# Seven FFN operand blocks at seven byte offsets: 128, 144, ... 224 behind a multiple of 256 in place of 192 for all

## The chip, the cores and the metric

The kernel runs on one core of a Trainium2 chip. The metric is the time of one execution on the device in microseconds (us). The operands lie in SBUF, the on-chip memory with 128 partitions; "an operand begins n bytes behind a multiple of 256" is said of its place within each partition. TensorE multiplies a stationary operand (128 x 128, the weights, loaded by an instruction of its own) by a moving one (128 partitions x 256 or 512 columns here) and adds the product up in PSUM. ScalarE (ACT in the profile) and VectorE (DVE) convert, add and multiply; GpSimd (POOL) and SyncE (SP) mostly issue DMAs.

## The reference, cut to what matters

One layer over 512 latent tokens of width 1024, behind a context of 256 tokens: a mixer (pooling and a two-way mLSTM), then a SwiGLU feed-forward network (FFN) of inner width 2816, then a last norm. The part in question is the FFN's first product:

```python
def _swiglu(h, w_in, w_out):
    g, u = jnp.split(h @ w_in, 2, axis=-1)
    return (jax.nn.silu(g) * u) @ w_out

x = x + g2 * _swiglu(_modulate(x, norm_ffn[l], sh2, sc2), w_ffn_in[l], w_ffn_out[l])
```

Here h is 512 x 1024 and w_in 1024 x 5632, all float32.

## The kernel before

Everything is kept transposed: features on the partitions (eight k tiles of 128), tokens in the columns, in two halves of 256. A float32 product is made of three matmuls of a faster type (float32r): each operand is split into a high part (a rounded copy) and a low one (the rest), and `mm3` (L180 to L186) issues, for each k tile, high weights by high tokens (L184), high weights by low tokens (L185) and low weights by high tokens (L186). The weights are the stationary operand, the tokens the moving one.

The FFN's inner width is cut into 22 blocks of 128 gate and 128 up columns. The first three blocks are computed directly (`Half`, L1126): for each half of the tokens, eight k tiles by three matmuls for the gate and as many for the up part. Blocks 3 to 21 go through a Strassen-Winograd scheme over 2 x 2 parts (gate and up by the two halves of the k tiles, and these by the two halves of the tokens): seven products in place of eight. `front` (L1046) and `back` (L1065) issue them, four k tiles by three matmuls each: twelve matmuls of 256 columns per product. `strassen` (L1080) interleaves the front of a block with the back of the block before; the weights of the next block are loaded, split and combined meanwhile by `prepare` (L997). In between, after blocks 7, 14 and 21, the second FFN product runs over the finished blocks (`ffn_out`, L1217), in matmuls of 512 columns, of 256 in the last round.

The moving operands of the Strassen products are the seven blocks that the change moves. B11, B21 and B22 are parts of the normed tokens (first half of the tokens with the upper and the lower four k tiles, second half with the lower four); N1, N2, T3 and T4 are sums and differences of such parts. Each is 128 x 1024, that is four k tiles of 256 columns, `kt(q, k)` (L944). All seven lie one behind the other in one tile, and there are two such tiles, `hp` (L940), one for the high parts and one for the low ones. `tl` aligns a tile to LINE = 256 bytes, and NEXT = 48 floats, 192 bytes, are left free at its beginning; a block is 4096 bytes long, so all seven, and each of their k tiles, begin 192 bytes behind a multiple of 256. The fourth part, B12, lies in tiles of its own (`act`, L1121) that begin on a multiple of 256. The direct blocks read the same operands: B11 and B21 for the first half of the tokens, B12 and B22 for the second (`hpart`, L947).

The blocks are written once, between the norm and the first Strassen product: B11, B21 and B22 by `norm_rest` (L957: ScalarE the high part at L960, VectorE the low one at L963), the others by `total` (L978) with casts and subtractions of 512 columns (`split`, L172). The order of TensorE's, ScalarE's and VectorE's work is written out by hand (`manual_schedule`), and nothing in it depends on where an operand begins. The filling matmuls before the last norm (`dense`, L1250) read B11 as both operands.

The stationary operands of the Strassen products are 128-column parts of the tiles wh, wl, gh, gl, oh and ol. All of these begin on multiples of 256 and a part is 512 bytes long, so the stationary operand always begins on a multiple of 256 there.

Of the kernel before, what the change touches and what calls it, by code (L numbers as in the profile page):

```python
# [11 lines left out]
F32R = mybir.dt.float32r  # L12
# [5 lines left out]
P = 128  # L18
D = 1024
# [13 lines left out]
LINE = 256  # L33
NEXT = 48
# [15 lines left out]
def layer_kernel(ctx: ExitStack, tc, xT, cT, w0, w1, wv0, wv, wada_a, wada_b, par, crow, bg, wpool,  # L50
# [17 lines left out]
    def tl(tag, shape, dtype=F32, bufs=1, align=None):  # L68
        cnt[0] += 1
        return homes[tag].tile(shape, dtype, name=f"{tag}_{cnt[0]}", tag=tag, bufs=bufs, align_bytes=align)  # L70
# [866 lines left out]

    hp = [tl("hp", [P, NEXT + 7 * D], F32R, 2, LINE) for _ in range(2)]  # L940
    B11, B21, B22, N1, N2, T3, T4 = ([t[:, NEXT + i * D:NEXT + (i + 1) * D] for t in hp] for i in range(7))
    B12 = None

    def kt(q, k):  # L944
# [429 lines left out]
```

## Time and profile before

| what | us |
|---|---|
| median of three timed runs | 891.28 |
| lowest and highest of them | 890.16, 891.31 |
| profiled execution, its own time | 892.56 |
| its span, first to last instruction | 890.8 |
| direct blocks 0 to 2 and writing of the hp tiles, about | 527 to 566 |
| Strassen products of blocks 3 to 7, with a change to the second FFN product after them | 566 to 618 |
| Strassen products of blocks 8 to 14 | 662.6 to 733 |
| Strassen products of blocks 15 to 21 | 770.5 to 839 |

The profile is of one execution. In its views, a group of instructions is given by line, engine, operation and tile (out<-in), with the number (x), the busy time, the mean duration of one in ns and the idle time before them. A timeline row has the start in us, the duration in us, engine, line, operation and tiles. The duration of a matmul reaches from its start to its modelled end; matmuls overlap, so the next one starts long before that, and what counts for the time is the distance from start to start, called the pace here. PEclk is the clock that TensorE was granted, in tenths of full speed on the page and as a share in the windows view.

### The profile page before, as it was taken

What the parts mean: (1) busy time and instruction counts of PE and PEld (TensorE: products, weight loads), DVE (VectorE), ACT (ScalarE), POOL (GpSimd) and SP (SyncE); (2) the same over time, 40 slices, a digit from 0 to 9 for tenths busy, and PEclk for the clock granted to TensorE, in tenths of its full rate; (3) what the DMA queues carried; (4) which work ended last, traced back from release to release, by engine and by line L of the source; (5) the groups of instructions that cost most, each with busy time, mean ns of one, the idle gap of its engine ahead of it and who ended that gap; (6) DMA issues with size and microseconds to landing.
All of it is one profiled execution on the core that took longest, in us unless ns stands there. A gap on an engine that the chain in (4) does not pass through costs nothing.

```text
span 890.8 us, 15038 instructions
## 1 busy us (share of the span) xinstructions
PE 879.4 (99%) x5920; PEld 801.3 (90%) x5920; DVE 613.4 (69%) x1187; ACT 434.7 (49%) x823; POOL 66.6 (7%) x93
## 2 busy tenths in 40 slices
PE   9999999999999999999999999999999999999996
PEld 7689798899888998889988899999889998899996
DVE  4678676868876787667886667884386743867644
ACT  4464363545345453354544456763156732666541
POOL 0000010010000100001000000110011100111000
PEclk9999999999999999999999999999999999999998
DMA  9853031435252632525343920574256643766402
GB/s 349 322 190 114 27 69 61 166 118 167 91 182 71 201 115 76 181 79 166 130 148 102 315 86 24 134 184 110 90 158 150 164 96 101 189 146 141 118 1 95
DMA packets 41445, 120.87 MB, mean 136 GB/s; under 512 B 4480, under 2 KB 8864, under 8 KB 40352
## 3 DMA queue, kind: packets, MB, share of 16 engines
q1 hardware_dynamic: 35904, 109.96, 38.2%
q0 software_dynamic: 5472, 9.96, 6.8%
q8 instruction: 46, 0.75, 0.3%
q14 instruction: 23, 0.19, 0.1%
HBM read 116.22 MB, written 3.69 MB: 135 GB/s over the span
## 4 chain that ended last, share of the span: by engine, by line
PE 89%; DVE 5%; ACT 3%; DMA 2%; issue 1%; DVEq 0%; SPq 0%; ACTq 0%
PE ps L184 20%; PE ps L186 20%; PE ps L185 20%; PE pat L334 3%; PE ps L566 3%; PE ps L565 3%; PE ps L567 3%; PE pat L781 2%; PE pat L780 2%; PE pat L779 2%; PE pat L184 2%; PE pat L185 2%; PE pat L186 2%; PE ps L334 1%; PE pat L740 1%; PE pat L739 1%
## 5 line engine op out<-in xcount | busy, mean ns | idle before, releaser
L184 PE MATMUL ps<-a,wh 128*128 128x512 f32 (+1 forms) x368 | 138.9, 377 | 0.0
L185 PE MATMUL ps<-a,wh 128*128 128x512 f32 (+1 forms) x368 | 138.5, 376 | 0.0
L186 PE MATMUL ps<-a,wl 128*128 128x512 f32 (+1 forms) x368 | 138.3, 376 | 0.0
L154 ACT CAST wh<-wr 128x1024 fp32r<-128x1024 f32 (+3 forms) x78 | 78.8, 1010 | 116.1 <-PE ps L185 88.2
L155 DVE TENSOR_TENSOR wl<-wr,wh 128x1024 fp32r<-128x1024 f32 (+3 forms) x78 | 91.8, 1177 | 44.4 <-ACT wh L154 43.3
L186 PEld LDWEIGHTS ps<-a,wl 128*128 128x128 f32 x368 | 69.3, 188 | 12.5
L184 PEld LDWEIGHTS ps<-a,wh 128*128 128x128 f32 x368 | 69.3, 188 | 12.2
L185 PEld LDWEIGHTS ps<-a,wh 128*128 128x128 f32 x368 | 69.3, 188 | 11.8
L186 PE MATMUL ps<-act,wl 128*128 128x512 f32 (+1 forms) x224 | 77.9, 348 | 0.6 <-DVE wl L155 0.6
L184 PE MATMUL ps<-act,wh 128*128 128x512 f32 (+1 forms) x224 | 77.9, 348 | 0.0
L185 PE MATMUL ps<-act,wh 128*128 128x512 f32 (+1 forms) x224 | 77.7, 347 | 0.0
L566 PE MATMUL ps<-wl,a 128*128 128x256 f32 (+1 forms) x192 | 54.5, 284 | 0.0
L567 PE MATMUL ps<-wh,a 128*128 128x256 f32 (+1 forms) x192 | 54.3, 283 | 0.0
L565 PE MATMUL ps<-wh,a 128*128 128x256 f32 (+1 forms) x192 | 54.3, 283 | 0.0
L1013 POOL DMA_DIRECT2D ol<-in_wffi x38 | 33.4, 888 | 258.0 <-ACT ol L1012 88.5
L184 PE MATMUL ps<-hp,gh 128*128 128x256 f32 x176 | 50.1, 285 | 1.2 <-ACT pat L1051 1.2
L1222 DVE SCALAR_TENSOR_TENSOR x<-ps,lb,x 128x512 f32<-128x512 f32 (+1 forms) x32 | 19.6, 616 | 45.6 <-PE ps L186 45.6
L184 PE MATMUL ps<-hp,oh 128*128 128x256 f32 x176 | 49.4, 280 | 0.1
L186 PE MATMUL ps<-hp,gl 128*128 128x256 f32 x176 | 49.2, 279 | 0.0
L185 PE MATMUL ps<-hp,gh 128*128 128x256 f32 x176 | 49.2, 279 | 0.0
L185 PE MATMUL ps<-hp,oh 128*128 128x256 f32 x176 | 49.1, 279 | 0.0
L186 PE MATMUL ps<-hp,ol 128*128 128x256 f32 x176 | 49.0, 279 | 0.0
(323 smaller groups left out, 2529.6 us busy)
## 6 DMA issues: line engine op xcount, KB each, us to landing
wr<-in_w SPq DMA_DIRECT2D x42, 512.0 KB, 3.5
pb<-in_wada_b SPq DMA_DIRECT2D x32, 512.0 KB, 4.2
wr<-in_wffi SPq DMA_DIRECT2D x25, 512.0 KB, 4.5
ur<-in_wffi SPq DMA_DIRECT2D x19, 512.0 KB, 3.9
ol<-in_wffi POOLq DMA_DIRECT2D x38, 256.0 KB, 4.9
ada<-in_wada_a SPq DMA_DIRECT2D x8, 1024.0 KB, 9.8
wr<-in_wffo SPq DMA_DIRECT2D x16, 448.0 KB, 3.5
wr<-in_wout SPq DMA_DIRECT2D x8, 512.0 KB, 3.5
```

What stands on the lines that cost most here:

```text
L154: nc.scalar.copy(wh, raw[:, :n])
L155: V.tensor_sub(wl, raw[:, :n], wh.bitcast(F32))
L184: nc.tensor.matmul(dst, wh, ah, start=first and i == 0, stop=False, skip_group_check=on)
L185: nc.tensor.matmul(dst, wh, al, start=False, stop=False, skip_group_check=on)
L186: nc.tensor.matmul(dst, wl, ah, start=False, stop=last and i == n - 1, skip_group_check=on)
L334: nc.tensor.matmul(acc0[i], w_first[k][i][w], aT[k][x], start=k + w + x == 0, stop=k == KT - 1 and w == 1)
L565: nc.tensor.matmul(acc[:, :n], ah, wh, start=kk == 0, stop=False)
L566: nc.tensor.matmul(acc[:, :n], ah, wl, start=False, stop=False)
L567: nc.tensor.matmul(acc[:, :n], al, wh, start=False, stop=kk == KT - 1)
L779: nc.tensor.matmul(o, sh_, vh[:, s, :], start=n == 0, stop=False)
L1013: nc.gpsimd.dma_start(l, dram, accum_op=ALU.add)
L1222: V.scalar_tensor_tensor(x1[j][:, c], acc[:, c], g2[:, j:j + 1], x1[j][:, c], ALU.mult, ALU.add)
```

## The change

The tile grows to 32 + 7 x 1028 floats, and block i begins at float 32 + 1028 i in place of 48 + 1024 i. In bytes that is 128 + 4112 i: with i from 0 to 6, B11 begins 128 bytes behind a multiple of 256, B21 144, B22 160, N1 176, N2 192, T3 208 and T4 224. The four k tiles of a block are 1024 bytes apart, so each has its block's offset. The high and the low tile change alike. Lengths, order, instructions and what is computed stay.

```diff
-    hp = [tl("hp", [P, NEXT + 7 * D], F32R, 2, LINE) for _ in range(2)]
-    B11, B21, B22, N1, N2, T3, T4 = ([t[:, NEXT + i * D:NEXT + (i + 1) * D] for t in hp] for i in range(7))
+
+    hp = [tl("hp", [P, 32 + 7 * (D + 4)], F32R, 2, LINE) for _ in range(2)]
+    B11, B21, B22, N1, N2, T3, T4 = ([t[:, o:o + D] for t in hp] for o in range(32, 7 * (D + 4), D + 4))
     B12 = None
```

## Prediction, on record before the result

> **What bounds the kernel now.** I read the page first: busy time, the clock in 40 slices, the chain that ended last.
>
> ```profile
> span 890.8 us, 15038 instructions
> PE 879.4 (99%) x5920; PEld 801.3 (90%) x5920; DVE 613.4 (69%) x1187; ACT 434.7 (49%) x823; POOL 66.6 (7%) x93
> PEclk9999999999999999999999999999999999999998
> PE 89%; DVE 5%; ACT 3%; DMA 2%; issue 1%; DVEq 0%; SPq 0%; ACTq 0%
> ```
>
> TensorE is busy 99% of the span, at the full granted clock, and 89% of the chain is its. A busy TensorE is not yet one at its best pace, though, so the second question is how far apart its matmuls start. The change touches only operands in the two hp tiles. The windows view, once for the matmuls that read hp and once for all matmuls in other stretches, gives length, busy time and (x) how many matmuls lie in each stretch:
>
> ```profile
> core 0: us, PE busy (x), PEclk, DMA share, GB/s
> 566.00:590.00 24.00, 22.80 (x192) 1.00 0.85 203
> 590.00:618.00 28.00, 28.00 (x240) 1.00 0.51 128
> 662.60:733.00 70.40, 69.92 (x588) 1.00 0.56 136
> 770.50:773.20 2.70, 2.67 (x23) 1.00 0.54 146
> 773.50:809.30 35.80, 35.80 (x312) 1.00 0.65 153
> 809.50:839.00 29.50, 29.50 (x252) 1.00 0.51 116
> ```
> ```profile
> 676.00:726.00 50.00, 50.00 (x427) 1.00 0.60 141
> 776.00:789.00 13.00, 13.00 (x117) 1.00 0.59 131
> 509.00:522.00 13.00, 13.00 (x111) 1.00 0.39 142
> 62.00:78.00 16.00, 16.00 (x129) 1.00 0.42 140
> ```
>
> And the groups of these stretches, by form, for the duration of one (in this order: 670 to 730, 776 to 789, 509 to 522, 62 to 78 us):
>
> ```profile
> L186 PE MATMUL ps<-hp,gl 128*128 128x256 f32 x48 | 13.5, 281 | 0.0
> L184 PE MATMUL ps<-hp,gh 128*128 128x256 f32 x12 | 3.3, 276 | 0.0
> L186 PE MATMUL ps<-act,ol 128*128 128x256 f32 x21 | 5.9, 283 | 0.0
> L566 PE MATMUL ps<-wl,a 128*128 128x272 f32 x43 | 12.5, 290 | 0.0
> ```
>
> A matmul is counted in a window when any part of it lies there, so with W the window and d one duration the pace is (W + d) / x. From 676 to 726 us: (50 + 0.281) / 427 = **117.8 ns**. From 776 to 789: (13 + 0.276) / 117 = **113.5 ns**. These are the same matmuls on the same operands (moving operand 192 bytes behind a multiple of 256, stationary one on the multiple); no wait lies in either. The duration tells the two apart: 281 ns against 276. From 509 to 522, where the moving operand is an act tile and begins on the multiple as the stationary one does: (13 + 0.283) / 111 = **119.7 ns**. So what bounds this stage is the pace, and the pace depends on where the operands begin, with two values for one and the same pair of places.
>
> When does it change? Around 809 us the pace turns from the fast to the slow one, at a matmul that started late:
>
> ```profile
> 809.19 0.28 PE L185 MATMUL ps<-hp,wh 128*128 128x256 f32 x1
> 809.31 0.28 PE L186 MATMUL ps<-hp,wl 128*128 128x256 f32 x1
> 809.43 0.38 PE L184 MATMUL ps<-hp,gh 128*128 128x256 f32 x1
> 809.65 0.28 PE L185 MATMUL ps<-hp,gh 128*128 128x256 f32 x1
> ```
>
> It starts 0.12 us after its forerunner, lasts 0.38, and the next comes 0.22 later. The stretch after it is slow, (29.5 + 0.281) / 252 = 118.2 ns with that stop. So the pace is held until something disturbs it, and the disturbance picks it anew.
>
> **The change part by part.** Nothing is added or taken away: the same instructions, semaphores and DMAs. In each hp tile block i of the seven moves from 192 bytes behind a multiple of 256 to 128 + 16 i. In a row's bytes the tile grows from 28,864 to 28,912; both round up to 113 x 256, so I take the tiles to begin where they did.
>
> First, the writes into hp (12 conversions of 256 columns and 8 casts of 512 on ScalarE, as many subtractions on VectorE). The same form into an act tile, on the multiple of 256, beside it:
>
> ```profile
> L960 ACT ACTIVATE hp<-tmp,lb 128x256 fp32r<-128x256 f32 x9 | 4.5, 495 | 0.0
> L960 ACT ACTIVATE act<-tmp,lb 128x256 fp32r<-128x256 f32 x4 | 2.0, 504 | 0.1
> L963 DVE SCALAR_TENSOR_TENSOR hp<-tmp,lb,hp 128x256 fp32r<-128x256 f32 x12 | 5.8, 483 | 0.4 <-ACT hp L960 0.3
> L963 DVE SCALAR_TENSOR_TENSOR act<-tmp,lb,act 128x256 fp32r<-128x256 f32 x4 | 1.9, 479 | 0.2 <-ACT act L960 0.2
> ```
>
> 495 against 504 and 483 against 479 ns: 9 ns either way over 20 writes is 0.2 us on an engine beside the path. Cost: nothing.
>
> Second, the matmuls. In the planned stage (blocks 3 to 21 of the first FFN product, 19 turns of seven products of twelve) 1596 matmuls read hp. Today one offset serves all seven products, so nothing but a stop disturbs a pace once taken. After the change the offset moves at every product: in the order of the trace B22 160, B21 144, T4 224, B11 128, N1 176, T3 208, N2 192, back to 160. The trace has one place where the offset moves every twelve matmuls at this width: the gate and up products of the second half, where the first four k tiles lie in act tiles (on the multiple) and the last four in hp (192 behind):
>
> ```profile
> 545.76 0.28 PE L186 MATMUL ps<-act,gl 128*128 128x256 f32 x1
> 545.88 0.29 PE L184 MATMUL ps<-hp,gh 128*128 128x256 f32 x1
> 546.00 0.28 PE L185 MATMUL ps<-hp,gh 128*128 128x256 f32 x1
> 546.12 0.28 PE L186 MATMUL ps<-hp,gl 128*128 128x256 f32 x1
> 546.24 0.28 PE L184 MATMUL ps<-hp,gh 128*128 128x256 f32 x1
> 546.35 0.28 PE L185 MATMUL ps<-hp,gh 128*128 128x256 f32 x1
> ...
> 547.26 0.28 PE L184 MATMUL ps<-act,gh 128*128 128x256 f32 x1
> ...
> 548.68 0.29 PE L184 MATMUL ps<-hp,gh 128*128 128x256 f32 x1
> ```
>
> The hp dozen takes 547.26 - 545.88 = 1.38 us, **115.0 ns** each: some starts 0.12 apart, then (546.35 to 547.26, eight starts) 0.91 / 8 = 113.8. The change of offset has brought it into the fast pace, at the cost of a few matmuls. The dozen on the multiple takes 548.68 - 547.26 = 1.42, 118.3 each, on its way to the 119.7 above.
>
> If every product after the change behaves as that hp dozen, the sum over the planned stage is: the slow matmuls, 240 + 588 + 23 + 252 = 1103, go from 117.8 to 115.0, 1103 x 2.8 = **3.1 us less**; the 312 of 773.5 to 809.3 go from 113.5 to 115.0, **0.5 us more**; the first 192, a mixture with stops, stay. Net **2.6 us less**. The bounds of the unknown: the six new offsets are in no row at this width. Below, every matmul at the fast pace with nothing lost at the changes: 1103 x 4.3 = 4.7 us less. Above, every matmul at the 119.7 of the operands that begin alike: 1103 x 1.9 + 312 x 6.2 + 192 x 3.4 (taking that mixture at 116.3) = 4.7 us more. I take the value between, from the hp dozen, since it is the nearest row: same width, same tile, same dozen.
>
> (The windows hold 1607 matmuls in all, since one that lies across an edge, or of the direct blocks before 566, is counted too.) The cover for a faster TensorE is there: in the stage that ran fast, the other engines had room.
>
> ```profile
> 770.00:809.00 39.00, 39.00 (x337) 38.44 (x336) 29.35 (x47) 26.46 (x47) 6.11 (x7) 1.00 0.65 155
> ```
>
> VectorE 29.35 and ScalarE 26.46 of 39 us; next to be late is ScalarE's copy at L1051, which TensorE waited for twice, 1.2 us in all, between 556 and 840 us:
>
> ```profile
> PE ps L184 <- ACT pat L1051: 1.2, 2, 0.9
> ```
>
> The 17 filling matmuls at L1253 use B11 for both operands and stay alike; 0.
>
> A rule that speaks against the whole change: the Trainium skill, page "TensorE: Matmul & The Clock Gate", section "Step-by-step: what each phase is for", has TensorE read SBUF through two independent ports, so that loading the next weights takes no read bandwidth from the running matmul. By that rule the place of the operands is of no account and the sum is 0. The trace speaks against it with its 119.7, 117.8 and 113.5 ns.
>
> **The time.** The profiled execution took 892.56 us for its span of 890.8; less 2.6 it is 889.96. It lies 1.28 above the median of the timed runs, 891.28, and I carry the difference over to that: 891.28 - 2.6 = **888.7 us**.
>
> **The rivals.**
>
> *Slower: the products never settle, or settle badly.* Each change of offset costs, and dozens are too short, or an offset such as 128 has only the pace of operands that begin alike. For it: where the offset moves every three matmuls (62 to 78 us, 272 columns) the pace is (16 + 0.290) / 129 = 126.3, against 113.5 x 272 / 256 = 120.6 for the fast pace at that width, 5.7 more and never settled; and the act dozens above went up from the fast pace. Against it: the hp dozens did settle. Price: 113.5 + 5.7 = 119.2 for all, 1103 x 1.4 + 312 x 5.7 + 192 x 2.9 = 3.9 us more, **895.2 us**; at 119.7 it is 4.7 more, 896.0. It decides when over half of the matmuls are slow: with the start of a dozen as above and the rest at 117.8, a product costs 115.0 + 8 x 4.3 / 12 = 117.9, no better than today's slow pace, and the 312 at 113.5 lose theirs: 312 x 4.4 = 1.4 us more, 892.7.
>
> *No change.* Half of the products settle fast and half slowly, or the offsets do not matter and only stops do. Pace (115.0 + 117.9) / 2 = 116.45: 1103 x 1.35 = 1.5 less, 312 x 2.95 = 0.9 more, **890.7 us**; if nothing depends on the offset, 891.3. For it: both paces occur on one offset. Against it: the three values above.
>
> *The change does not do what it says.* If the tile did not begin on a multiple of 256, the offsets would be others; the row grows within its rounding, so I give this no chance of its own.
>
> **How the numbers follow.** Settling fast, 888.7 us: 0.42, by itself 886.6 (891.28 - 4.7, nothing lost at the changes) to 889.5. No change: 0.26. Slower: 0.32. A measurement of this kernel can tell about 0.2%, 1.8 us, from no change, so faster means under 889.5, slower over 893.1: 0.42, 0.26, 0.32. Cases of both signs hold most of the chance, so the range reaches from 886.3 to 895.8 and leaves some 0.05 out below and 0.10 above.
>
> **What would show it.** In the groups by form, the durations of the hp matmuls in the planned stage: 276 after the first few of each dozen if I am right, 281 or 283 in whole products if the rival is. Product by product, the start of one dozen to the start of the next: 1.36 to 1.38 us if fast, 1.41 slow, 1.44 as with operands that begin alike. If long stretches of all seven products keep 117.8 as they do now, the change of offset does not pick the pace anew, and the mechanism is wrong. More waits for L1051 than 1.2 us would show that the gain is spent there.

## The result: 892.88 us, slower by 0.34%

| | median us | lowest, highest | runs |
|---|---|---|---|
| kernel before, beside the changed one | 890.09 | 888.98, 891.31 | 7 |
| changed kernel | 892.88 | 892.53, 894.13 | 7 |

The ratio is 1.0034, with a 95% interval from 1.0022 to 1.0046. The profiled execution of the changed kernel took 892.77 us, its span 891.0. That is only 0.21 us more than the profiled execution of the kernel before, 892.56: the 2.79 us stand between the medians, and why the two profiles lie so near to each other comes out further down.

The page of the changed kernel, the lines that answer to those shown of before:

```profile
span 891.0 us, 15038 instructions
PE 880.9 (99%) x5920; PEld 803.4 (90%) x5920; DVE 613.7 (69%) x1187; ACT 435.6 (49%) x823; POOL 66.8 (7%) x93
PEclk9999999999999999999999999999999999999999
PE 91%; DVE 4%; ACT 2%; issue 2%; DMA 0%; DVEq 0%; POOLq 0%; POOL 0%; ACTq 0%
```

Same number of instructions, same granted clock: the distances between the matmuls' starts are left to explain, that is the pace and the stops. The windows of the planned stage, for the matmuls that read hp (length, busy time, number), as in the prediction:

```profile
566.00:590.00 24.00, 23.41 (x198) 1.00 0.86 217
590.00:618.00 28.00, 27.34 (x232) 1.00 0.46 116
662.60:733.00 70.40, 68.78 (x580) 1.00 0.56 134
676.00:726.00 50.00, 50.00 (x427) 1.00 0.59 139
773.50:809.30 35.80, 35.80 (x305) 1.00 0.65 149
811.00:833.00 22.00, 22.00 (x189) 1.00 0.48 109
```

From 773.5 to 809.3 us the profile of before had 312 matmuls, this one has 305: that stretch went from 113.5 ns to about 118. From 676 to 726 nothing changed (427 and 427), because before had 117.8 there. From 566 to 590 the changed kernel even fits in six more, 198 for 192: TensorE was busy with them for 23.41 us there and for 22.80 before, so it lost less to stops. By the next stage it was 1.1 us ahead (first matmul at 661.45, before at 662.59), which is why 590 to 618 and 662.6 to 733 count fewer.

One turn of the changed kernel, the first matmul of each product from the timeline (B11, N1, T3, N2, then N2's seventh matmul, B22, B21, T4 and the next B11), each with its own offset:

```profile
677.49 0.28 PE L184 MATMUL ps<-hp,oh 128*128 128x256 f32 x1
...
678.93 0.28 PE L184 MATMUL ps<-hp,gh 128*128 128x256 f32 x1
...
680.35 0.28 PE L184 MATMUL ps<-hp,wh 128*128 128x256 f32 x1
...
681.78 0.28 PE L184 MATMUL ps<-hp,gh 128*128 128x256 f32 x1
...
682.49 0.28 PE L184 MATMUL ps<-hp,gh 128*128 128x256 f32 x1
...
683.17 0.28 PE L184 MATMUL pat<-hp,wh 128*128 128x256 f32 x1
...
684.58 0.28 PE L184 MATMUL pat<-hp,oh 128*128 128x256 f32 x1
...
685.98 0.28 PE L184 MATMUL ps<-hp,oh 128*128 128x256 f32 x1
...
687.40 0.28 PE L184 MATMUL ps<-hp,oh 128*128 128x256 f32 x1
```

Differences of the starts give the dozens. The rows round a start to 0.01 us; the table has the dozens to the nanosecond, from the same trace:

| product | B11 | N1 | T3 | N2 | B22 | B21 | T4 |
|---|---|---|---|---|---|---|---|
| bytes behind the multiple | 128 | 176 | 208 | 192 | 160 | 144 | 224 |
| us per dozen | 1.437 | 1.425 | 1.425 | 1.392 | 1.409 | 1.399 | 1.419 |
| ns per matmul | 119.8 | 118.8 | 118.8 | 116.0 | 117.4 | 116.6 | 118.3 |

The turn takes 687.40 - 677.49 = 9.91 us, **118.0 ns** per matmul. Only N2, the one product still at 192, does what the prediction hoped for all seven: its first six matmuls take 682.49 - 681.78 = 0.71 us (118), its last six 0.68 (113).

### The profile page after: what moved, and what is told of

The parts are those of the page before. It is cut to its first block, busy times and chain, and to the rows that moved or that the text cites. A ratio compares the mean times of both kernels' runs of the same rounds, so it can differ in the third digit from the quotient of the medians.

```text
span 891.0 us, 15038 instructions
## 1 busy us (share of the span) xinstructions
PE 880.9 (99%) x5920; PEld 803.4 (90%) x5920; DVE 613.7 (69%) x1187; ACT 435.6 (49%) x823; POOL 66.8 (7%) x93
## 4 chain that ended last, share of the span: by engine, by line
PE 91%; DVE 4%; ACT 2%; issue 2%; DMA 0%; DVEq 0%; POOLq 0%; POOL 0%; ACTq 0%
PE ps L184 20%; PE ps L186 20%; PE ps L185 20%; PE pat L334 3%; PE ps L565 3%; PE ps L566 3%; PE ps L567 3%; PE pat L781 2%; PE pat L185 2%; PE pat L184 2%; PE pat L186 2%; PE pat L779 2%; PE pat L780 2%; PE ps L334 1%; PE pat L739 1%
## 5 line engine op out<-in xcount | busy, mean ns | idle before, releaser
L154 ACT CAST wh<-wr 128x1024 fp32r<-128x1024 f32 (+3 forms) x78 | 78.8, 1011 | 116.6 <-PE ps L185 88.7
```

The costliest lines, as they stand in the source:

```text
L154: nc.scalar.copy(wh, raw[:, :n])
```

## The experiments

Theory A: where the moving operand begins against the stationary one decides the pace a matmul settles at, and of the offsets in use only 192 can have 113.3 ns (1.36 us for a dozen start to start; the windows give it as 113.5). Rival B: any offset is as good, and the switching every twelve matmuls costs. Rival C: not the pace but waits moved the time. Later came two more: rival D (behind a change of offset the pace is a matter of chance) and rival E (the moving operand's place alone counts).

In the table, x is the number of hp matmuls in the window from 676 to 726 us, and the pace (50 + 0.28) / x, with the few stops in it. The table is followed by that window's row for each kernel, a fence each, in the order of the table.

| kernel | x | pace ns | time of it / of before, us | ratio, interval |
|---|---|---|---|---|
| all_64 | 426 | 118.0 | 893.11 / 889.96 | one run |
| all_128 | 423 | 118.9 | 894.48 / 891.43 | 1.0035, 1.0022 to 1.0048 |
| all_144 | 424 | 118.6 | 893.57 / 891.43 | 1.0025, 1.0016 to 1.0034 |
| all_176 | 422 | 119.1 | 895.67 / 891.43 | 1.0048, 1.0034 to 1.0061 |
| all_224 | 424 | 118.6 | 894.55 / 889.96 | one run |
| only_t4_160 | 433 | 116.1 | 890.63 / 891.43 | 0.9991, 0.9983 to 1.0000 |
| only_t4_0 | 436 | 115.3 | 889.70 / 889.96 | 0.9996, 0.9987 to 1.0005 |
| only_t4_208 | 436 | 115.3 | 889.34 / 889.96 | 0.9993, 0.9984 to 1.0002 |
| gh_192 | 424 | 118.6 | 895.00 / 889.68 | 1.0061, 1.0044 to 1.0078 |
| before_a | 438 | 114.8 | 888.57 / 889.68 | one run |
| before_b | 439 | 114.5 | 887.87 / 889.68 | one run |
| after_a | 426 | 118.0 | 893.79 / 889.68 | one run |

```profile
676.00:726.00 50.00, 50.00 (x426) 1.00 0.60 140
```
```profile
676.00:726.00 50.00, 50.00 (x423) 1.00 0.60 141
```
```profile
676.00:726.00 50.00, 50.00 (x424) 1.00 0.59 140
```
```profile
676.00:726.00 50.00, 50.00 (x422) 1.00 0.62 143
```
```profile
676.00:726.00 50.00, 50.00 (x424) 1.00 0.61 141
```
```profile
676.00:726.00 50.00, 50.00 (x433) 1.00 0.60 139
```
```profile
676.00:726.00 50.00, 50.00 (x436) 1.00 0.59 139
```
```profile
676.00:726.00 50.00, 50.00 (x436) 1.00 0.60 141
```
```profile
676.00:726.00 50.00, 50.00 (x424) 1.00 0.61 143
```
```profile
676.00:726.00 50.00, 50.00 (x438) 1.00 0.62 140
```
```profile
676.00:726.00 50.00, 50.00 (x439) 1.00 0.61 144
```
```profile
676.00:726.00 50.00, 50.00 (x426) 1.00 0.58 141
```

One more thing can be read from all fourteen profiles, the first two included. Add up the planned stage from its first to its last hp matmul in its three stretches: that gives 184.9 (before_a) to 191.9 us (all_176). What is left of each execution's time lies between 702.8 and 703.9 us in every one. So the differences arise in the planned stage, and not in a tile elsewhere that the edits might have shifted.

### One offset for all seven, another than 192

Each kernel differs from the one before in the two numbers of the layout (32, 36, 44, 16 and 56 floats for 128, 144, 176, 64 and 224 bytes):

```diff
-    hp = [tl("hp", [P, NEXT + 7 * D], F32R, 2, LINE) for _ in range(2)]
-    B11, B21, B22, N1, N2, T3, T4 = ([t[:, NEXT + i * D:NEXT + (i + 1) * D] for t in hp] for i in range(7))
+    hp = [tl("hp", [P, 32 + 7 * D], F32R, 2, LINE) for _ in range(2)]
+    B11, B21, B22, N1, N2, T3, T4 = ([t[:, 32 + i * D:32 + (i + 1) * D] for t in hp] for i in range(7))
```

all_128: 

> All seven blocks begin 128 bytes behind a multiple of 256. Theory A (each offset of the moving operand against the stationary one has a pace of its own; only 192 has the pace of 113.3 ns): the planned stage runs at 119 to 120 ns throughout, duration 283, as the dozens of B11 did in the changed kernel (1.44 us per dozen); 1596 matmuls x (119.7 - 116.4) = 5.3 us more than before, ratio about 1.006. Rival B (it is the switching from one offset to another every twelve matmuls that costs, and any single offset keeps 113.4 or 117.8): pace 113.4 or 117.8, ratio 0.997 to 1.002. Rival C (the pace is not what moved the median; waits did): ratio near 1.000, whatever the pace.

all_144: 

> All seven blocks begin 144 bytes behind a multiple of 256. In the changed kernel B21 at this offset took 116.6 ns per matmul in the steady turns, and once, after a stop, 113.4. Theory A: the stage settles at one or the other: ratio 1.000 if 116.6, 0.995 if 113.4. Rival B: 113.4 or 117.8 with changes at stops, ratio 0.995 to 1.002. Rival C: ratio near 1.000.

all_176: 

> All seven blocks begin 176 bytes behind a multiple of 256. Theory A: pace 118.8 ns throughout, as the dozens of N1 in the changed kernel (1.425 us per dozen), in a pattern that repeats over several matmuls; 1596 x 2.4 = 3.8 us more, ratio about 1.004. Rival B: 113.4 or 117.8, ratio 0.997 to 1.002. Rival C: ratio near 1.000.

all_64: 

> All seven at 64. A look at the paces of one more offset, also a multiple of 64 bytes as 0, 128 and 192 are. Theory A: a pace of its own between 113.3 and 119.7, held over whole turns; if multiples of 64 other than the stationary operand's place are alike, 113.3 and 117.8 as at 192; if 64 is like 0 and 128, about 119.

all_224: 

> All seven at 224. In the changed kernel T4 at this offset took 118.2 ns per matmul. Theory A: 118 to 118.8 over whole turns, 281 to 284 ns durations mixed, time some 3 us above the kernel before beside it. Rival B (a single offset holds 113.4 or 117.8): durations 276 or 281 alone.

No switching is left in these kernels, and yet three of them are slower than before clear of their intervals, and the single runs of the other two lie above all 21 runs of before beside them (highest 892.22). Rival B falls as the reason for the loss, and with it rival C, since the time follows the pace. (Switching does cost a little: N2's dozen in the changed kernel takes 1.392 us, 32 ns more than twelve at 113.3.) Theory A stands in its core: none of the five offsets ran this window at 113 to 115 ns. The offsets 160 and 208 were not run for all seven. In detail it was off. At 144 there are two paces on one offset, as there are at 192: 118.6 in the window of the table, and later, from the windows view of the same kernel,

```profile
811.00:833.00 22.00, 22.00 (x191) 1.00 0.50 112
```

(22 + 0.28) / 191 = 116.6, the pace that B21 had in the changed kernel. The 113.4 foreseen as an alternative did not come; nor did any dozen of B21 in the changed kernel have it, the shortest took 1.399 us, 116.6 ns each. At 128 it was 118.9, not 119.7: a pattern of 115 to 122 ns that repeats every five matmuls or so. And 64 held 118.0, a value rival B also allows, but never the lower one.

### One product alone elsewhere

The six others stay at 192; for 160 and 0, T4 is put first in the tile (40 or 0 floats) and the six behind it, for 208 last:

```diff
-    B11, B21, B22, N1, N2, T3, T4 = ([t[:, NEXT + i * D:NEXT + (i + 1) * D] for t in hp] for i in range(7))
+    B11, B21, B22, N1, N2, T3, T4 = ([t[:, o:o + D] for t in hp] for o in (1072, 2096, 3120, 4144, 5168, 6192, 40))
```

only_t4_160: 

> Only T4 begins elsewhere (160 bytes behind a multiple of 256), the other six stay at 192. Theory A: T4's dozen takes about 117.5 ns per matmul, and the next dozen (B11, 192) falls into 113.3 after some five matmuls as N2's did in the changed kernel, and stays there for all six: per turn 12 x 4.2 + 26 = 76 ns over the pace of 113.3, 19 turns 1.4 us, against some 1596 x 3.1 = 4.9 us in the kernel before: 3.5 us less, ratio about 0.996, durations of 276 in nearly all dozens but T4's. Rival B: two switches a turn in place of seven cost two sevenths of what the change costs, and between them the pace stays at what it was, 113.4 or 117.8: ratio 0.999 to 1.002. Rival C: ratio near 1.000.

The expectation missed. T4 every 84 matmuls does pick the pace of the six products behind it anew, but where no stop comes between it picks the two values turn about. The first matmuls of T4 and of B11 behind it, two turns of this kernel from its timeline (T4 at 686.29 and 695.89):

```profile
677.82 0.28 PE L184 MATMUL ps<-hp,oh 128*128 128x256 f32 x1
...
686.29 0.28 PE L184 MATMUL ps<-hp,oh 128*128 128x256 f32 x1
...
687.72 0.28 PE L184 MATMUL ps<-hp,oh 128*128 128x256 f32 x1
...
695.89 0.28 PE L184 MATMUL ps<-hp,oh 128*128 128x256 f32 x1
```

The 72 matmuls from 677.82 to 686.29 take 117.6 ns each, the 72 from 687.72 to 695.89 take 113.5. The changed offset hands something on, and what it hands on depends on how it was entered. That gave the next two kernels, with an offset that has a single pace (0), and with one that stood ahead of 192 in the changed kernel (208).

only_t4_0: 

> Only T4 begins elsewhere, on the multiple of 256 (offset 0), the other six at 192. With T4 at 160 the six dozens behind it took 113.5 and 117.8 ns turn about: the pace of T4's dozen in its last matmuls decides which one follows. Theory A with this addition (a dozen on another offset hands on a place in time, and the next offset falls into the pace that belongs to it): offset 0 has a single pace, 119.7, as 509 to 522 us of the kernel before, so each turn hands on the same place; in the direct blocks of before, a dozen at 192 behind one at 0 fell into 113.3 every time. So all turns but those behind 512-column matmuls run their six at 113.3: per turn 61 ns in T4's dozen and some 20 in the next, 19 x 0.08 = 1.5 us over the pace of 113.3 against some 5.3 before: 3.5 us less, ratio about 0.996. Rival D (the pace behind a change is picked at random, or turn about, whatever the offset): as with 160, ratio about 0.999.

only_t4_208: 

> Only T4 begins elsewhere, at 208. In the changed kernel N2 (192) stood behind T3 (208) and fell into 113.3 after five or six matmuls in every turn looked at. Theory A with the addition: the same here, per turn 12 x 5.5 + 32 = 98 ns, 1.9 us over the pace of 113.3: 3.3 us less than before, ratio about 0.996 to 0.997, unless T4's dozen, which here comes from 192 and not from 176, ends otherwise. Rival D: ratio about 0.999.

The mechanism came as theory A had it, against rival D: 115.3 ns in the window for both, where 160 had 116.1. In only_t4_0 a turn without a stop:

```profile
714.49 0.28 PE L184 MATMUL ps<-hp,oh 128*128 128x256 f32 x1
...
715.91 0.29 PE L184 MATMUL ps<-hp,oh 128*128 128x256 f32 x1
...
724.09 0.28 PE L184 MATMUL ps<-hp,oh 128*128 128x256 f32 x1
```

T4's dozen takes 1.42 us and the 72 behind it 8.18, 113.6 ns. Not every turn ran so: a stop inside a turn could bring the higher pace until the next T4, as in only_t4_0 from 702.05 to 704.88 us, 24 matmuls at 117.8 ns. And the time did not follow: 3.3 to 3.5 us less were expected and 0.3 and 0.6 measured, neither clear of no change. One reading is that the kernel before, in the runs beside these, was not at 117.8 for three quarters of the stage as it was in its profile. That was tried next.

### The kernel before, twice more

before_a: 

> The kernel before once more (a blank line at its end). Theory A says that with one offset for all the pace behind each stop is a matter of the moment of the stop, so its share of 113.3 and 117.8 by stage differs from execution to execution: in the first profile some 0.75 of the planned stage was at 117.8; here anything from 0.3 to 1, in stretches that end at stops. If the shares are the same to within 5%, the stops fall alike every time and the two medians of before (891.4 and 890.0 us in two groups of runs) come from something else.

before_b: 

> The kernel before a third time (two blank lines at its end), to see with the run beside it how far the shares of 113.3 and 117.8 differ: theory A as there, anything from 0.3 to 1 at 117.8; its rival, the same share in all three profiles to within 5%.

after_a: 

> The changed kernel once more (a blank line at its end). Theory A: it forgets the moment of a stop within a turn or two, so each offset's dozen takes the same time as in the first profile (B11 1.437, N1 1.425, T3 1.425, N2 1.392, B22 1.409, B21 1.399, T4 1.419 us) and the mean of the planned stage is 117.9 ns again to within 0.2. If the means differ by 1 ns or more, the changed kernel picks its pace at stops too.

From the groups of 670 to 730 us, first before_a and then after_a, one row each:

```profile
L184 PE MATMUL ps<-hp,oh 128*128 128x256 f32 x48 | 13.2, 276 | 0.0
```
```profile
L186 PE MATMUL ps<-hp,gl 128*128 128x256 f32 x48 | 13.4, 279 | 0.0
```

and the windows from 773.5 and 811 us, before_a and then after_a:

```profile
773.50:809.30 35.80, 35.80 (x313) 1.00 0.64 143
811.00:833.00 22.00, 22.00 (x196) 1.00 0.48 106
```
```profile
773.50:809.30 35.80, 35.80 (x303) 1.00 0.62 147
811.00:833.00 22.00, 22.00 (x189) 1.00 0.49 112
```

The same kernel that had a duration of 281 and 117.8 ns from 670 to 730 us in its first profile has 276 and 114.8 here, and (22 + 0.28) / 196 = 113.7 ns in the last stretch, where it had 118. Its three profiled executions took 892.56, 888.57 and 887.87 us. The highest less the lowest is 4.7 us, and the 1103 matmuls of the first profile that stood at 117.8 cost 1103 x 4.3 ns = 4.7 us over 113.5: the pace accounts for the spread. This is the range that the timed runs of before have too (887.86 to 892.38 in the groups here). The groups ran on different chips, with medians of 891.43, 889.96 and 889.68; but the second group has 887.86 to 892.22 on one chip, so the spread is not one between chips alone.

The expectation for the two repeats missed all the same. From 0.3 to 1 of the stage was to be at 117.8, and about 0.05 was: of some 113 dozens without a stop, 3 in before_a and 2 in before_b. That the share differs between executions is shown (0.75 against these); that each execution draws it afresh is not, since the two repeats are alike and both from the same chip.

A lower pace is not all gain. In before_a and before_b 29 and 28 matmuls of the stage start 126 ns or more after the one before, and these stops come to 3.5 and 3.7 us over the pace; in the two profiles of the changed kernel there are 10 and 11, and 1.8 and 2.0 us. So some 1.7 us of what the lower pace saves is lost in stops. In part these are waits for ScalarE and VectorE: between 556 and 840 us the profiles name 2.0 and 2.3 us of such waits there, and 1.0 us in both of the changed kernel.

The changed kernel gave the same count of matmuls within 2 in three of its windows in both profiles (427 and 426, 305 and 303, 189 and 189 in the last), as expected. No stop sets its pace for long; it is at some 118 ns in both.

### The weights moved in place of the tokens

gh and gl begin 192 bytes behind a multiple of 256; hp stays:

```diff
-        return tl(tag, [P, D], F32R, bufs, LINE)
+        return tl(tag, [P, NEXT + D], F32R, bufs, LINE)[:, NEXT:]
```

gh_192: 

> hp stays at 192; the weights tiles gh and gl, the stationary operands of the products with N1 and N2 (and of direct block 0), begin 192 bytes behind a multiple of 256 too. Theory A (what counts is where the two operands begin against each other): the dozens with N1 and N2 now take 118.4 to 119.7 ns per matmul, as T4 at 0 against weights at 0 did (1.42 us per dozen, pattern 119 113 117 118 119 121 117 117 120 120 120 120 or its like), and the product behind each starts 121 122 115 115 and falls to 113.3; per turn about 2 x 81 ns over the pace of 113.3, ratio 0.998 to 1.001. Rival E (the place of the moving operand alone counts): N1 and N2 keep 113.3 or 117.8, as in the kernel before, ratio 1.000.

One dozen with gh and the next with wh, from the timeline of this kernel:

```profile
680.54 0.28 PE L184 MATMUL ps<-hp,gh 128*128 128x256 f32 x1
...
681.98 0.28 PE L184 MATMUL ps<-hp,wh 128*128 128x256 f32 x1
...
683.39 0.28 PE L184 MATMUL ps<-hp,gh 128*128 128x256 f32 x1
```

The gh dozen takes 1.44 us, 120.0 ns per matmul, as operands that both begin on the multiple do, although the moving operand stands at 192 as ever. Rival E falls: the two places count against each other. The second half of the expectation missed: the dozen behind it, at 192 against 0, takes 1.41, 117.5, and not the lower pace that followed T4 at 0; why is open. Nearly all of the stage stays at 118 to 120. The ratio of 1.0061, where 0.998 to 1.001 was expected, is the highest of all, though its interval overlaps that of all_176. The edit also moves gh and gl where the output projection and the last round of the second FFN product use them; outside the planned stage this kernel takes 703.9 us, at most 1.1 more than any other, so that is not what made it slower by 5.3.

## Why the prediction was wrong, point by point

- **Bound by TensorE's pace, pace set by the operands' places, two paces on one pair of places, picked at a disturbance:** right for 192, and 144 showed two paces too, 118.6 and 116.6. The profiles of 64, 128, 176 and 224 show one pace each.
- **Writes into hp cost nothing, tiles begin where they did, same instructions:** right for the writes and the instructions, 15038 in both; where a tile begins is in no trace. In the changed profile the ScalarE conversions into hp take 498 ns on average and VectorE's subtractions 480, in the profile before 498 and 483.
- **A change of offset picks the pace anew:** right, see the T4 kernels.
- **"I take the value between, from the hp dozen, since it is the nearest row":** this is the step that failed. The row is of offset 192, and it was taken for seven offsets. For 192 it held (N2: 1.39 us for 1.38). The other six took 1.40 to 1.44, so the mean is 118.0 ns and not 115.0. In the prediction's own sum that is (1103 + 312) x 3.0 = 4.2 us, as much as lies between the 888.7 forecast and the 892.88 measured. That it closes so well is luck, since the next term was off as well, and so was the stops' share, which the sum left as it was.
- **"1103 go from 117.8 to 115.0":** the base was mis-sized too. These matmuls stood at 117.8 in the profiled execution; in the two later profiles of the same kernel nearly all stood at 113.5. The text saw that the profiled execution lay 1.28 us above the median, and above every timed run then shown, and carried that over as a constant. It had far more of the higher pace than the two later ones, and in executions like those there is less to gain than the sum said, and more to lose.
- **The rival with a slower end** named the mechanism (an offset such as 128 has no good pace) and, in its last sentence, the pace: 117.9 ns for all, the lower pace lost. Its 892.7 us for the 892.88 measured is in part luck: it is 1.4 more than 891.28, and the changed kernel took 2.79 more than the kernel before beside it, whose median was 890.09. Its dearer forms are 3.9 and 4.7 us more, at 119.2 and 119.7 ns; all_176 comes near them, with 119.1 ns and 4.2 us more than before beside it.
- **More waits for L1051 if TensorE gets faster:** it did not, and the changed kernel's wait for this copy (L1052 there, the same line one further down) is 0.6 us, for 1.2 before. At 113.5 the gain is spent in part in other, shorter stops: 50.28 / 113.5 would be 443 matmuls from 676 to 726 us, before_b has 439, so some 0.5 us of 50, and over the whole stage the 1.7 us above.
- **The rule of the Trainium skill** (page "TensorE: Matmul & The Clock Gate", section "Step-by-step: what each phase is for": two independent read ports, by which the prediction's rival took the place of the operands to be of no account): by it nothing would have changed. The ratio of 1.0034, and 1.0061 with nothing but the weights tiles gh and gl moved, speak against that conclusion for float32r matmuls with 256 columns. Whether reading is what makes the difference, no run here shows.

Still open: why these places against each other give these paces, what picks one of the two at 192 behind a stop, and what share of the higher pace an execution of the kernel before usually has, since the timed runs show no paces. No kernel here tells that apart. No version was found that is clear of the kernel before: only_t4_160 comes nearest, at 0.9991 with 0.9983 to 1.0000.

## What to carry to other kernels

When TensorE is busy all the time, measure the distance from start to start and not the busy time, by stretches, and look whether one and the same instruction has two paces. If it has, one profile is one draw: take two or three of the kernel before predicting from its share, and distrust a profiled execution that lies above all the timed ones. Part of a better pace is lost again in stops. And a row at one offset is a row at that offset alone; before spreading operands over seven, run each by itself.

## What the runs showed of the hardware

A 128 x 256 float32r matmul with its own weights load settled at 113.5 ns at best and at about 120 with both operands equally far behind a multiple of 256 (120.0 in gh_192 at 192 and 192, 119.7 with act tiles at 0 and 0); at 192 against 0 it takes 113.5 or 117.8 and keeps either for hundreds of matmuls. Shifts of 16 bytes are enough: 176, 192 and 208 gave 118.8, 116.0 and 118.8 in the same turn. The whole effect, 113.5 to 120, is 6% of a matmul. The two paces at 192 alone, 113.5 and 117.8, made 4.7 us of 890 between profiled executions of one unchanged kernel.
